# Moving GLU, gates and a branch between attention heads, and building SSM rotations from tables

## The chip, the cores and the metric

The kernel runs on one core of one Trainium2 chip. The time is device microseconds of one launch, from runs that each compute the whole layer; lower is better. A profile is one further execution, recorded by the hardware profiler. Engines are named as in the profile: PE (TensorE, matmuls), PEld (its weight loads), DVE (VectorE), ACT (ScalarE), POOL (GpSimd), SP (SyncE, which here issues most DMAs).

## The reference

One layer of a decoder over 1024 tokens with 16 meta tokens ahead of them (1040 positions, width 1024), all in float32:

```
xn = RMSNorm(h);  [q | k | v | u | gate_a | gate_b] = xn @ W_in
a  = stick-breaking attention(q, k, v)     8 heads x 64, strictly causal
     z = q.k / 8;  w[t,s] = sigmoid(z[t,s]) * prod over s<j<t of sigmoid(-z[t,j]);  a = w @ v
y  = gelu(S5(u))                           32 groups x 16 channels, 64 complex states each
     x_t = lam x_(t-1) + B u_t;  S5 = Re(C x_t) + D u_t
s  = y * sigmoid(y @ W_glu + b)
h += (sigmoid(gate_a) * (a @ W_pa) + sigmoid(gate_b) * (s @ W_pb)) @ W_o
h += MoE(RMSNorm(h))                       top 1 of 4 groups, top 2 of its 8 experts
out = RMSNorm(h), meta tokens dropped
```

## The kernel before

**Matmuls in two parts.** Operands are split into a rounded high part (type float32r) and the rest as a low part. `split` (L99) makes both: a cast on ACT and a subtraction on DVE. `mm3` (L132) then does three matmuls, high by high, high by low, low by high. `load_w` (L144) loads a block of weights through a buffer `wr` (two of them) and splits it; the parts go to `wh` and `wl`, two buffers each.

**Order of the work.** A tile framework orders the instructions of each engine ahead of time by a simulated timeline, and follows the order of the program as a priority; what runs on the chip is that fixed order with semaphores. The program is written with generators. `weave(main, fill, n_main, n_fill)` (L57) takes one step of the main work and then so many of the fill that both come out even; `drain` runs one to its end. The stages, in the order of the program:

- The norm of all 1040 positions gives `xh` and `xl` (the transposed input in two parts, 66 KB a partition together), which stay until the last projection is done. `ssm_in` projects `u` and sends it to memory.
- `ssm_prep` (L370) computes on DVE, in many small operations of 32 elements, the powers of the state's decay, the tables `BA`, `BB`, `C1`, `C2`, and `c`, `s`: cosine and sine of the angle of eight steps.
- `ssm` (L515) handles four blocks of eight groups. The sequence is cut into chunks of eight positions, so a state runs over 129 chunk steps. A block's rotations `RC`, `RS` (cosine and sine of 0 to 128 such angles) are built on POOL by doubling: seven rounds of six products and sums (L549 to L554). Then DVE builds `GT` and `ET`, PE transposes and multiplies (L569, L577), SP copies `KP` into the eight shifted bands of `M`, PE multiplies the input (L598), DVE rotates the result with `RC` and `RS` (L600 to L603), scans it (L606), POOL and DVE rotate it back (L608 to L611), PE makes the output (L618, L620), which goes through a gelu to memory (`y_d`).
- `gates` (L176) is 16 projections in 32 steps, each 24 matmuls of 512 columns, a sigmoid and a store to `gate_d`. Twenty-one steps are woven into the SSM's 24 (SF = 21), three stand after it (MF = 3), the other eight among the first three head pairs (GP = 3, 3, 2).
- Attention works on four pairs of heads. `att_proj` (L669) projects q, k and v of a pair in eight steps. For q the 64 rows of a head are followed by the 64 rows of its low part, so `qs` has 128 rows; the high part of k stands twice in `k1`, its low part twice in `k2`. `att_pair` (L727) has 16 steps: two heads, four double blocks of queries, two steps each. A chunk of scores is two matmuls over 128 rows (L745 with `k1`, L746 with `k2`); then two sigmoids on ACT, masks on POOL (L751), the running product on DVE (L754), the weights on POOL (L755), transposes on PE (L770), a split, and the product with V (L790; L785 in the last pair, without low parts). The 16 meta tokens are a key block of their own, with matmuls of 16 rows. Into each of the first three pairs the next pair's projection and the gate steps are woven.
- The last pair takes its first step, then the remaining gate steps run, `xh` and `xl` are freed, and `glu` (L632) is woven into the pair: it loads `y_d`, splits it, does eight products of 12 matmuls and writes the parts of s to `sh`, `sl`. The attention's results of the other pairs are loaded from memory (`attn_d`) into `ah`, `al`.
- The branch loop (L334) does, for each of eight column blocks, the SSM's part (24 matmuls), the attention's part (24) and the products with the gates. Then come the output projection with the router, and 32 experts.

Of the kernel before, what the change touches and what calls it, by code (L numbers as in the profile page):

```python
# [44 lines left out]
SF, MF, GP = 21, 3, (3, 3, 2)  # L45
# [28 lines left out]
def tile_block(ctx, tc, i, out):  # L74
# [64 lines left out]
    with ExitStack() as ca:  # L139
# [21 lines left out]
        with ExitStack() as cx:  # L161
# [120 lines left out]
            next(pair)  # L282
            drain(gen)
            cq.close()


        with ExitStack() as c4:
# [3 lines left out]
            with ExitStack() as c6:  # L291
                nc.sync.dma_start(gb, i["glu_b"])
                at = pool(c6, "glu", bufs=2, side="right")
                gl = glu(tc, at, ps, i, load_w, mm3, split, gb, y_d, sh, sl)

                def loads():
                    for k in range(3):
                        a = wp.tile([128, 2, 512], F32, name="wr", bufs=2)
                        nc.sync.dma_start(a, attn_d[k * 128:k * 128 + 128])
                        split(ah[:, k], al[:, k], a.rearrange("p a b -> p (a b)"))  # L300
                        yield
# [32 lines left out]
            for m in range(KD):  # L334
                h, l = load_w([wb[:, :, m * 128:m * 128 + 128], wa[:, :, m * 128:m * 128 + 128]])
                T2 = []
                for q in range(2):
                    c = slice(q * 512, q * 512 + 512)
                    t = ps.tile([128, 512], F32, name="qk", bufs=2)
                    for k in range(4):  # L340
                        mm3(t, h[:, k, :], l[:, k, :], sh[:, k, c], sl[:, k, c], k == 0, k == 3)
# [28 lines left out]
def ssm_prep(tc, p, i, bcast, out):  # L370
# [144 lines left out]
def ssm(tc, p, ps, ident, u_d, y_d, prep):  # L515
# [9 lines left out]
    for blk in range(4):  # L525
# [876 lines left out]
```

## Time and profile before

| | |
|---|---|
| three runs, median (lowest to highest) | 1538.57 us (1536.74 to 1539.53) |
| the profiled execution, its own time | 1539.6 us |
| its span, first to last instruction | 1537.7 us |
| mean granted clock of TensorE | 0.974 |
| DVE, ACT, POOL busy | 63%, 47%, 34% |
| SSM stage, about | 73 to 272 us |
| four head pairs, about | 285 to 652 us |
| branch, output projection, router | 655 to 864 us |
| experts and the end | 864 to 1538 us |

The profile's matmuls overlap (the end of one is modelled), so the distance between two starts says what a matmul costs, not its length. A row of the timeline gives its start, its length, the engine, line and operation, what it writes and reads with its size, how many like it follow, and in brackets the engine's idle time before it and what ended it. `128*128 128x512` is a matmul of 128 rows by 128 columns of weights, with 128x512 moving elements.

### The profile page before, as it was taken

To read this page: it belongs to the slowest core of one execution; us is meant where nothing else is said; L and a number is where in the kernel's file an instruction comes from. 1 tells how busy PE (TensorE), PEld (TensorE's weight loads), DVE (VectorE), ACT (ScalarE), POOL (GpSimd) and SP (SyncE) were. 2 spreads that over 40 slices of the span, in tenths; PEclk is the share of its full clock that TensorE was granted. 3 is DMA by queue.
4 is the path that set the end of the run, shared out by engine and by line. 5 is a ranking of instruction groups with operands and counts; after the bars stand their busy time and mean duration, and the time that the engine had idled before them with its cause. 6 is when DMAs were issued, how large, how long until landed. Compare 5 with 4: busy or idle time off the path is not lost. (4 is left out here: it accounts for less than half of the span.)

```text
span 1537.7 us, 19509 instructions
## 1 busy us (share of the span) xinstructions
PE 1456.8 (95%) x6900; PEld 1123.4 (73%) x6900; DVE 963.0 (63%) x1488; ACT 722.3 (47%) x1141; POOL 518.9 (34%) x542
## 2 busy tenths in 40 slices
PE   7989799999999989999998799999999999999986
PEld 6967688998888867778787566666666666666663
DVE  6757565465756568665578566666665566656547
ACT  6212122455656577432223255555555455555543
POOL 1199941144444465332255321111111111111034
PEclk8999899999999999999999799999999999999998
DMA  8242344211111015264763799999999989999754
GB/s 256 77 104 72 92 104 97 60 42 54 30 51 34 28 44 142 78 198 160 268 247 124 286 346 356 352 354 353 356 360 351 353 342 358 334 334 357 271 200 163
DMA packets 132197, 314.77 MB, mean 205 GB/s; under 512 B 24305, under 2 KB 82289, under 8 KB 107522
## 3 DMA queue, kind: packets, MB, share of 16 engines
q1 hardware_dynamic: 120898, 295.99, 55.0%
q0 software_dynamic: 9728, 16.83, 2.9%
q8 instruction: 55, 0.90, 0.2%
q10 hardware_dynamic: 1472, 0.69, 0.2%
q14 instruction: 44, 0.36, 0.1%
HBM read 284.03 MB, written 44.11 MB: 213 GB/s over the span
## 5 line engine op out<-in xcount | busy, mean ns | idle before, releaser
L134 PE MATMUL mm<-xh,wh 128*128 128x512 f32 (+4 forms) x608 | 224.1, 369 | 1.1 <-DVE kl L691 0.6
L135 PE MATMUL mm<-xl,wh 128*128 128x512 f32 (+4 forms) x608 | 222.6, 366 | 0.0
L136 PE MATMUL mm<-xh,wl 128*128 128x512 f32 (+4 forms) x608 | 221.3, 364 | 0.8 <-DVE wl L102 0.8
L1159 POOL DMA_INDIRECT ye_d<-w,tab x32 | 56.1, 1754 | 250.0 <-ACT w L1152 249.4
L134 PEld LDWEIGHTS mm<-xh,wh 128*128 128x128 f32 x608 | 115.4, 190 | 16.0 <-issue 1.1
L136 PEld LDWEIGHTS mm<-xh,wl 128*128 128x128 f32 x608 | 115.4, 190 | 14.9 <-DVE wl L102 1.5
L135 PEld LDWEIGHTS mm<-xl,wh 128*128 128x128 f32 x608 | 115.3, 190 | 13.9 <-DVE xl L225 0.4
L754 DVE TENSOR_TENSOR_SCAN pr<-pr 128x144 f32<-128x144 f32 (+3 forms) x64 | 92.6, 1448 | 46.8 <-POOL pr L751 46.1
L102 DVE TENSOR_TENSOR w<-m,w 128x2048 fp32r<-128x2048 f32 x38 | 88.9, 2342 | 40.8 <-ACT w L101 40.7
L102 DVE TENSOR_TENSOR w<-r,w 128x2048 fp32r<-128x2048 f32 x36 | 82.2, 2291 | 47.6 <-ACT w L101 47.2
L1066 POOL DMA_INDIRECT w<-hg_d,tab x31 | 34.8, 1122 | 222.0 <-PE tr L1088 217.1
L755 POOL TENSOR_TENSOR be<-be,pr 128x143 f32<-128x143 f32 (+3 forms) x64 | 89.4, 1400 | 38.4 <-DVE pr L754 36.0
L1120 PE MATMUL a<-r,xf 128*128 128x512 f32 x224 | 100.7, 592 | 0.0
L1120 PE MATMUL a<-m,xf 128*128 128x512 f32 x208 | 93.3, 592 | 0.0
L1128 DVE SCALAR_TENSOR_TENSOR mid<-a,tab,mid 128x512 f32<-128x512 f32 x64 | 47.9, 749 | 63.8 <-ACT mid L1126 52.0
L101 ACT CAST w<-r 128x2048 fp32r<-128x2048 f32 x38 | 72.1, 1903 | 27.5 <-PE a L1113 14.4
L101 ACT CAST w<-m 128x2048 fp32r<-128x2048 f32 x38 | 72.5, 1907 | 18.9 <-PE o L1146 10.3
L101 ACT CAST wh<-wr 128x1024 fp32r<-128x1024 f32 (+1 forms) x44 | 44.6, 1014 | 65.8 <-PE mm L135 57.3
L1120 PEld LDWEIGHTS a<-r,xf 128*128 128x128 f32 x224 | 41.8, 190 | 42.3 <-issue 40.4
L102 DVE TENSOR_TENSOR wl<-wr,wh 128x1024 fp32r<-128x1024 f32 (+1 forms) x44 | 57.1, 1297 | 23.6 <-ACT wh L101 23.5
L1146 PE MATMUL o<-w,w 128*128 128x512 f32 x172 | 68.6, 399 | 3.2 <-DVE w L102 3.2
L751 POOL TENSOR_SCALAR_AFFINE_SELECT pr<-pr 128x128 f32<-128x128 f32 x64 | 26.3, 411 | 132.9 <-ACT pr L748 113.1
(534 smaller groups left out, 3766.2 us busy)
## 6 DMA issues: line engine op xcount, KB each, us to landing
r<-in_w_dram SPq DMA_DIRECT2D x84, 1024.0 KB, 7.9
m<-in_w_dram SPq DMA_DIRECT2D x82, 1024.0 KB, 8.1
x<-in_w_dram SPq DMA_DIRECT2D x26, 1024.0 KB, 7.9
wr<-in_w_in_dram SPq DMA_DIRECT2D x32, 512.0 KB, 4.2
gate_d<-gt SPq DMA_DIRECT2D x32, 256.0 KB, 2.3
x<-in_x_dram SPq DMA_DIRECT2D x8, 512.0 KB, 4.6
y<-y_d SPq DMA_DIRECT2D x16, 256.0 KB, 3.2
wr<-in_w_out_dram SPq DMA_DIRECT2D x8, 512.0 KB, 4.3
```

The source lines that it names most:

```text
L101: a = (A if heng is None else heng).copy(h, src)
L102: return a.ins, (V if leng is None else leng).tensor_sub(l, src, _f(h)).ins
L134: nc.tensor.matmul(ps, lhsT=wh, rhs=xh, start=first, stop=False)
L135: nc.tensor.matmul(ps, lhsT=wh, rhs=xl, start=False, stop=False)
L136: nc.tensor.matmul(ps, lhsT=wl, rhs=xh, start=False, stop=last)
L754: V.tensor_tensor_scan(rv, rv, rv, 1.0, op0=OP.mult, op1=OP.bypass)
L755: P.tensor_mul(be[:, :W - 1], be[:, :W - 1], pr[:, 1:W])
L1066: q = P.indirect_dma_start(out=xg[e % XG], out_offset=None, in_=hg_d, in_offset=IO(ap=tab[:, e, 0:1] if e else rt["idx"], axis=0), bounds_ ...
L1120: nc.tensor.matmul(a[w], lhsT=xf[:, k], rhs=raws[n][:, k], start=False, stop=(k == 3))
L1128: V.scalar_tensor_tensor(s, a[n], r, s, op0=OP.mult, op1=OP.mult)
L1146: nc.tensor.matmul(o[n], lhsT=hh[:, kk], rhs=l[:, k, cs], start=False, stop=False)
L1159: put = P.indirect_dma_start(out=ye_d, out_offset=IO(ap=tab[:, e, 1:2], axis=0), in_=y, in_offset=None, bounds_check=2 * S - 1, oob_is_err ...
```

## The change

It does five things. The GLU runs earlier: it is loaded in the middle of the first pair's projection, and its eight products are the first fill of the first pair, followed by the second pair's projection and one gate step (17 fill steps in 16); its result goes to memory (`s_d`) instead of `sh`, `sl`. The three gate steps between the SSM and attention go; pairs 0, 1 and 2 have 1, 3 and 3, and the first half of the last pair has four (GL). In the second half of the last pair s is loaded and split, and the SSM's part of the first two column blocks is done (AHEAD = 2), with products of the gates kept in `gb`; the branch loop starts the others itself. The low part of k is kept once, each head in its own 64 rows, and L746 multiplies it with the 64 rows of q's high part, so the product of the two low parts is no longer formed. The rotations come from two tables made once in `ssm_prep`, `pb` (0 to 16 angles) and `pa` (0 to 8 times 16 angles), by one complex product over 8 x 9 x 16 elements a block: the sine's three operations on DVE, the cosine's three on POOL. Beside that, `M` is two tiles cleared once, `KP` has half its size, `ET` one buffer in place of two, and the first head's result of the last pair goes through `attn_d`.

```diff
-SF, MF, GP = 21, 3, (3, 3, 2)
+SF, GP, GL = 21, (1, 3, 3), 4
+AHEAD = 2
...
+    s_d = dr.tile([512, S], F32, name="s_d")
...
-            aq = [None, pool(c3, "aq1", bufs=2)]
-            cq = ExitStack()
-            aq[0] = pool(cq, "aq0", bufs=2)
+            aq = [pool(c3, "aq0", bufs=2), None]
+            cg = ExitStack()
+            nc.sync.dma_start(gb, i["glu_b"])
+            gl = glu(tc, pool(cg, "glu", bufs=2, side="right"), ps, i, load_w, mm3, split, gb, y_d, s_d)
             st = {}
-            drain(islice(gen, MF), att_proj(tc, ap, aq[0], ps, proj, ident, 0, st))
+            pr0 = att_proj(tc, ap, aq[0], ps, proj, ident, 0, st)
+            drain(islice(pr0, 4))
+            next(gl)
+            drain(pr0)
+
+            def ahead():
+                yield from gl
+                cg.close()
+                aq[1] = pool(c3, "aq1", bufs=2)
+                yield from att_proj(tc, ap, aq[1], ps, proj, ident, 1, st)
+
             for hp in range(3):
                 pair = att_pair(tc, ap, ps, ident, hp, st, attn_d)
-                fill = chain(att_proj(tc, ap, aq[(hp + 1) % 2], ps, proj, ident, hp + 1, st), islice(gen, GP[hp]))
-                weave(pair, fill, 16, 8 + GP[hp])
+                nx = ahead() if hp == 0 else att_proj(tc, ap, aq[(hp + 1) % 2], ps, proj, ident, hp + 1, st)
+                fill = chain(nx, islice(gen, GP[hp]))
+                weave(pair, fill, 16, 8 + GP[hp] + (8 if hp == 0 else 0))
                 drain(fill, pair)
+
             dst = []
             pair = att_pair(tc, ap, ps, ident, 3, st, attn_d, dst)
-            next(pair)
+            weave(pair, gen, 8, GL)
             drain(gen)
-            cq.close()
+            cx.close()
...
-            with ExitStack() as c6:
-                nc.sync.dma_start(gb, i["glu_b"])
-                at = pool(c6, "glu", bufs=2, side="right")
-                gl = glu(tc, at, ps, i, load_w, mm3, split, gb, y_d, sh, sl)
...
-                dst += ah, al
-                weave(pair, chain(gl, loads()), 16, 18)
-                drain(pair, gl)
+            pg = pool(c5, "gat", side="right", bufs=2)
+            wa = i["w_branch_attn"].rearrange("(k p) c -> p k c", p=128)
+            wb = i["w_branch_ssm"].rearrange("(k p) c -> p k c", p=128)
+            wu, parts = {}, {}
+
+            def load_s(src, h_, l_, k, n):
+                a = wp.tile([128, 2, 512], F32, name="wr", bufs=2)[:n]
+                nc.sync.dma_start(a, src[k * 128:k * 128 + n])
+                split(h_[:n, k], l_[:n, k], a.rearrange("p a b -> p (a b)"))
+
+            def ssm_part(m, nm):
+                wu[m] = load_w([wb[:, :, m * 128:m * 128 + 128], wa[:, :, m * 128:m * 128 + 128]])
+                h, l = wu[m]
+                for q in range(2):
+                    c = slice(q * 512, q * 512 + 512)
+                    g_ = parts[m, q] = pg.tile([128, 512], F32, name="gb", bufs=2 + 2 * AHEAD)
+                    nc.sync.dma_start(g_, gate_d[D + m * 128:D + m * 128 + 128, c])
+                    t = ps.tile([128, 512], F32, name=nm, bufs=2)
+                    for k in range(4):
+                        mm3(t, h[:, k, :], l[:, k, :], sh[:, k, c], sl[:, k, c], k == 0, k == 3)
+                    V.tensor_mul(g_, g_, t)
+                    yield
+
+            def early():
+                for k in range(4):
+                    load_s(s_d, sh, sl, k, 128)
+                    yield
+                for m in range(AHEAD):
+                    yield from ssm_part(m, "mm")
+                for k in range(3):
+                    load_s(attn_d, ah, al, k, 128)
+                    yield
+                load_s(attn_d, ah, al, 3, 64)
+                yield
+
+            dst += ah, al
+            fill = early()
+            weave(pair, fill, 8, 8 + 2 * AHEAD)
+            drain(pair, fill)
...
+                if m >= AHEAD:
+                    drain(ssm_part(m, "qk"))
+                h, l = wu[m]
...
+                    ga, g_ = pg.tile([128, 512], F32, name="ga"), parts[m, q]
...
+    f1, f2 = BA[:, :, 0:8], BA[:, :, 8:16]
+
+    def powers(nm, top, r1, i1):
+        R, I = W(nm + "r", (128, G, top + 1)), W(nm + "i", (128, G, top + 1))
+        V.memset(R[:, :, 0:1], 1.0)
+        V.memset(I[:, :, 0:1], 0.0)
+        V.tensor_copy(R[:, :, 1], r1)
+        V.tensor_copy(I[:, :, 1], i1)
+        n = 1
+        while n < top:
+            a, b = f1[:, :, :n], f2[:, :, :n]
+            ar, ai = R[:, :, 1:n + 1], I[:, :, 1:n + 1]
+            br, bi = (x[:, :, n:n + 1].to_broadcast([128, G, n]) for x in (R, I))
+            V.tensor_mul(a, ai, bi)
+            V.tensor_mul(b, ar, br)
+            V.tensor_sub(R[:, :, n + 1:2 * n + 1], b, a)
+            V.tensor_mul(a, ar, bi)
+            V.tensor_mul(b, ai, br)
+            V.tensor_add(I[:, :, n + 1:2 * n + 1], a, b)
+            n *= 2
+        return R, I
+
+    pb = powers("pb", 16, c, s)
+    pa = powers("pa", 8, pb[0][:, :, 16], pb[1][:, :, 16])
...
-        RC, RS = W("RC", (128, 8, N), bufs=2), W("RS", (128, 8, N), bufs=2)
-        P.memset(RC[:, :, 0:1], 1.0)
-        P.memset(RS[:, :, 0:1], 0.0)
-        P.tensor_copy(RC[:, :, 1], c[:, gs])
-        P.tensor_copy(RS[:, :, 1], s[:, gs])
-        ta, tb = W("ta", (128, 8, 64)), W("tb", (128, 8, 64))
-        n = 1
-        while n < 128:
-            br, bi = (x[:, :, n:n + 1].to_broadcast([128, 8, n]) for x in (RC, RS))
-            ar, ai = RC[:, :, 1:n + 1], RS[:, :, 1:n + 1]
-            a, b = ta[:, :, :n], tb[:, :, :n]
-            P.tensor_mul(a, ai, bi)
-            P.tensor_mul(b, ar, br)
-            P.tensor_sub(RC[:, :, n + 1:2 * n + 1], b, a)
-            P.tensor_mul(a, ar, bi)
-            P.tensor_mul(b, ai, br)
-            P.tensor_add(RS[:, :, n + 1:2 * n + 1], a, b)
-            n *= 2
+
+        RC, RS = (W(n, (128, 8, 9, 16), bufs=2) for n in ("RC", "RS"))
+        ta, tb = W("ta", (128, 8, 9, 16)), W("tmp", (128, 8, 9, 16))
+        (ar, ai), (br, bi) = ([x[:, gs, :9, None].to_broadcast([128, 8, 9, 16]) for x in pa],
+                              [x[:, gs, None, :16].to_broadcast([128, 8, 9, 16]) for x in pb])
+        for eng, R, t, x, y, op in ((V, RS, tb, (ar, bi), (ai, br), OP.add), (P, RC, ta, (ar, br), (ai, bi), OP.subtract)):
+            eng.tensor_mul(R, *x)
+            eng.tensor_mul(t, *y)
+            eng.tensor_tensor(R, R, t, op=op)
+        RC, RS = (x.rearrange("p g a b -> p g (a b)")[:, :, :N] for x in (RC, RS))
...
-        GT, tmp, ET = W("GT", (128, 8, T + 1, CH), bufs=2), W("tmp", (128, 8, T + 1, CH)), W("ET", (128, 8, T, CH), bufs=2)
+        GT, tmp, ET = W("GT", (128, 8, T + 1, CH), bufs=2), W("tmp", (128, 8, T + 1, CH)), W("ET", (128, 8, T, CH))
...
-        M = W("M", (128, 8, 128), bufs=2)
-        KPf = KP.rearrange("p g a b -> p g (a b)")
+        V.tensor_add(KP[:, :, 0:CH], KP[:, :, 0:CH], dg)
+        M = Ms[blk % 2]
         for ti in range(T):
-            nc.sync.dma_start(M[ti * CH:ti * CH + CH], KPf[:, :, 128 - CH * ti:256 - CH * ti])
+            nc.sync.dma_start(M[ti * CH:ti * CH + CH, :, CH * ti:], KP[:, :, :128 - CH * ti])
...
-            split(sh[:, m, c], sl[:, m, c], sg.rearrange("p c t -> p (c t)"))
+            nc.sync.dma_start(s_d[m * 128:m * 128 + 128, q * 512:q * 512 + 512], sg.rearrange("p c t -> p (c t)"))
...
-        k2 = [pq.tile([128, L], F32R, name="kl", bufs=2) for _ in range(2)]
+        k2 = pq.tile([128, L], F32R, name="kl", bufs=1)
...
-                V.tensor_sub(k2[e][a, n0:n1], t[a, :n], _f(k1[e][a, n0:n1]))
-                V.tensor_sub(k2[e][b, n0:n1], t[a, :n], _f(k1[e][a, n0:n1]))
+                V.tensor_sub(k2[a, n0:n1], t[a, :n], _f(k1[e][a, n0:n1]))
...
+            own = slice(64 * e, 64 * e + 64)
...
-                        nc.tensor.matmul(z[:, :c1 - c0], lhsT=q, rhs=k2[e][:, c0:c1], start=False, stop=True)
+                        nc.tensor.matmul(z[:, :c1 - c0], lhsT=q[own], rhs=k2[own, c0:c1], start=False, stop=True)
...
-                c = slice(j * 256, j * 256 + 256)
-                if dst is None:
-                    ao = p.tile([64, 256], F32, name="ao")
-                    A.copy(ao, po[64:128, :])
-                    V.tensor_add(ao, po[0:64, :], ao)
-                    nc.sync.dma_start(attn_d[(2 * hp + e) * 64:(2 * hp + e) * 64 + 64, c], ao)
+                c, row = slice(j * 256, j * 256 + 256), (2 * hp + e) * 64
+                if dst:
+                    ah, al = dst
+                    A.copy(ah[own, hp, c], po[own])
+                    V.tensor_sub(al[own, hp, c], po[own], _f(ah[own, hp, c]))
                 else:
-                    ah, al = dst
-                    r = slice(64 * e, 64 * e + 64)
-                    A.copy(ah[r, hp, c], po[r])
-                    V.tensor_sub(al[r, hp, c], po[r], _f(ah[r, hp, c]))
+                    ao = p.tile([128, 256], F32, name="ao")[own if dst is not None else slice(0, 64)]
+                    if dst is None:
+                        A.copy(ao, po[64:128, :])
+                        V.tensor_add(ao, po[0:64, :], ao)
+                    else:
+                        A.copy(ao, po[own])
+                    nc.sync.dma_start(attn_d[row:row + 64, c], ao)
```

## Rows read from the trace of the kernel before

**Rows 1.** Page, engines: busy us (share of the span) and instructions.
```profile
PE 1456.8 (95%) x6900; PEld 1123.4 (73%) x6900; DVE 963.0 (63%) x1488; ACT 722.3 (47%) x1141; POOL 518.9 (34%) x542
```

**Rows 2.** Windows by stage: length, busy us per engine, granted clock, DMA share, GB/s.
```profile
54.70:102.00 47.30, 47.30 (x245) 41.56 (x244) 40.54 (x152) 10.20 (x16) 27.75 (x38) 1.00 0.33 102
73.40:272.00 198.60, 180.38 (x892) 147.98 (x891) 123.90 (x162) 45.84 (x71) 134.37 (x197) 0.94 0.41 97
108.50:121.00 12.50, 5.56 (x16) 4.61 (x16) 7.88 (x15) 0.00 (x0) 11.17 (x26) 0.59 0.17 32
170.10:186.00 15.90, 5.92 (x30) 5.93 (x30) 3.54 (x4) 0.81 (x2) 14.83 (x29) 0.57 0.11 33
272.00:545.00 273.00, 270.07 (x1605) 237.99 (x1604) 168.44 (x251) 156.87 (x385) 112.42 (x135) 1.00 0.14 41
545.00:572.00 27.00, 21.28 (x113) 16.46 (x114) 17.30 (x26) 17.16 (x49) 18.03 (x24) 0.87 0.12 38
572.00:655.00 83.00, 79.88 (x393) 62.49 (x392) 59.89 (x57) 50.46 (x117) 36.80 (x36) 1.00 0.36 106
```

**Rows 3.** Timeline of TensorE, SSM stage: start, length, instruction, idle time before.
```profile
115.45 0.77 PE L598 MATMUL qk<-U,E 128*128 128x129 f32 x2 [6.94 <-DVE mm__1124 L602]
...
180.10 0.77 PE L618 MATMUL qk<-R,GT 128*128 128x128 f32 x2 [9.98 <-DVE R L611]
```

**Rows 4.** Timeline of VectorE, just before those two.
```profile
110.64 0.56 DVE L600 TENSOR_TENSOR R<-qk,RC 128x387 f32<-128x387 f32 x1 [8.53 <-POOL RC L551]
...
178.66 1.29 DVE L611 SCALAR_TENSOR_TENSOR R<-mm__1464,nsgn,R 128x1032 f32<-128x1032 f32 x1 [12.79 <-POOL R L608]
```

**Rows 5.** Lines of GpSimd, 67 to 207 us: count, busy us, mean ns, idle.
```profile
L551 POOL TENSOR_TENSOR RC<-tb,ta 128x8 f32<-128x8 f32 (+6 forms) x28 | 21.6, 773 | 2.0
...
L552 POOL TENSOR_TENSOR ta<-RC,RS 128x8 f32<-128x8 f32 (+6 forms) x28 | 16.6, 593 | 2.0
L608 POOL TENSOR_TENSOR R<-St,RC 128x1032 f32<-128x1032 f32 x2 | 4.8, 2396 | 0.0
```

**Rows 6.** Lines of VectorE by form, 54 to 102 us.
```profile
L558 DVE TENSOR_TENSOR GT<-C,Lr 128x1152 f32<-128x1152 f32 x2 | 2.7, 1356 | 0.0
...
L503 DVE TENSOR_TENSOR BA<-X,fr 128x512 f32<-128x512 f32 x1 | 0.7, 684 | 0.0
...
L454 DVE TENSOR_TENSOR Li<-t,t 128x128 f32<-128x128 f32 x1 | 0.3, 291 | 0.0
...
L454 DVE TENSOR_TENSOR Li<-t,t 128x32 f32<-128x32 f32 x1 | 0.2, 200 | 0.0
```

**Rows 7.** Timeline of TensorE around one matmul of 16 rows.
```profile
352.27 0.40 PE L136 MATMUL mm<-xh,wl 128*128 128x512 f32 x1
352.50 0.39 PE L134 MATMUL mm<-xh,wh 128*128 128x512 f32 x1
352.82 0.38 PE L790 MATMUL pv<-wth,V 16*128 16x256 f32 x1
353.13 0.51 PE L135 MATMUL mm<-xl,wh 128*128 128x512 f32 x1
353.48 0.40 PE L136 MATMUL mm<-xh,wl 128*128 128x512 f32 x1
```

**Rows 8.** Lines of VectorE, whole span.
```profile
L691 DVE TENSOR_TENSOR kl<-mm,kh 64x344 fp32r<-64x344 f32 (+1 forms) x24 | 12.4, 516 | 0.3
...
L102 DVE TENSOR_TENSOR al<-wr,ah 128x1024 fp32r<-128x1024 f32 x3 | 4.5, 1491 | 1.6 <-ACT ah L101 1.6
```

**Rows 9.** DMA issues, 540 to 660 us: count, KB each, us to landing.
```profile
wr<-attn_d SPq DMA_DIRECT2D x3, 512.0 KB, 3.4
```

**Rows 10.** Lines of TensorE, 276 to 655 us.
```profile
L746 PE MATMUL qk<-kl,qs 128*128 128x264 f32 (+6 forms) x112 | 36.2, 326 | 0.0
```

**Rows 11.** Timeline of TensorE around a transpose of 16 columns.
```profile
367.78 0.27 PE L770 MATMUL tr<-ident,be 128*16 128x128 f32 x1
367.80 0.36 PE L790 MATMUL pv<-wtl,V 128*128 128x256 f32 x1
```

More of the change, by code (lines that the diff above doesn't have):

```diff
@@ L159, in tile_block @@
         ei = con.tile([128, 128], I32, name="ei")
-        with ExitStack() as cx:
+        cx = ExitStack()
+        if True:
             xp = pool(cx, "xp", side="right")
@@ L290, in tile_block @@
             ah, al, sh, sl = (p.tile([128, 4, S], F32R, name=n) for n in ("ah", "al", "sh", "sl"))
-            with ExitStack() as c6:
-                nc.sync.dma_start(gb, i["glu_b"])
-                at = pool(c6, "glu", bufs=2, side="right")
-                gl = glu(tc, at, ps, i, load_w, mm3, split, gb, y_d, sh, sl)
[L296 to L301, printed above, removed]
-                dst += ah, al
-                weave(pair, chain(gl, loads()), 16, 18)
-                drain(pair, gl)
+            pg = pool(c5, "gat", side="right", bufs=2)
@@ L353, in tile_block @@
                     V.tensor_mul(ga, ga, t)
-                    P.tensor_add(ga, ga, gb)
+                    P.tensor_add(ga, ga, g_)
                     for r in range(2):
@@ L442, in ssm_prep @@
     V.tensor_mul(Li[:, 1], mag, s)
-    t1, t2 = W("t1", (128, 4, G)), W("t2", (128, 4, G))
+    BA, BB = (W(n, (128, G, CH)) for n in ("BA", "BB"))
+    t1, t2 = (BB.rearrange("p g c -> p (g c)")[:, n * 4 * G:(n + 1) * 4 * G].rearrange("p (a g) -> p a g", a=4) for n in range(2))
     n = 1
@@ L489, in ssm_prep @@
     yield
-    X, X2, C1, C2, BA, BB, u1 = (W(n, (128, G, CH)) for n in ("X", "X2", "C1", "C2", "BA", "BB", "u1"))
+    X, X2, C1, C2, u1 = (W(n, (128, G, CH)) for n in ("X", "X2", "C1", "C2", "u1"))
     for x, x2, src in ((X, X2, i["b"]), (C1, C2, i["c"])):
@@ L510, in ssm_prep @@
     V.tensor_scalar(C2, C2, -1.0, None, op0=OP.mult)
-    out.update(c=c, s=s, Lr=Lr, Li=Li, d8=d8, BA=BA, BB=BB, C1=C1, C2=C2, sg=sg, nsg=nsg, dd=dd)
+    out.update(pa=pa, pb=pb, Lr=Lr, Li=Li, d8=d8, BA=BA, BB=BB, C1=C1, C2=C2, sg=sg, nsg=nsg, dd=dd)
 def ssm(tc, p, ps, ident, u_d, y_d, prep):
@@ L517, in ssm @@
     V, A, P = nc.vector, nc.scalar, nc.gpsimd
-    c, s, Lr, Li, d8, BA, BB, C1, C2, sg, nsg, dd = (
-        prep[n] for n in ("c", "s", "Lr", "Li", "d8", "BA", "BB", "C1", "C2", "sg", "nsg", "dd"))
+    pa, pb, Lr, Li, d8, BA, BB, C1, C2, sg, nsg, dd = (
+        prep[n] for n in ("pa", "pb", "Lr", "Li", "d8", "BA", "BB", "C1", "C2", "sg", "nsg", "dd"))
     def W(name, shape=(128, G), dt=F32, bufs=1):
@@ L524, in ssm @@
     N = NCH - 1
+    Ms = [W(f"M{n}", (128, 8, 128)) for n in range(2)]
+    for M in Ms:
+        P.memset(M, 0.0)
     for blk in range(4):
@@ L570, in ssm @@
             A.copy(E[:, g0:g0 + 4], tp)
-        KP = W("KP", (CH, 8, 2, 128))
-        P.memset(KP[:, :, 0], 0.0)
+        KP = W("KP", (CH, 8, 128))
         for g0 in (0, 4):
@@ L629, in ssm, with glu @@
                                         ap=[[S, CH], [CH * S, 8], [1, 128]]), Y[ti * CH:ti * CH + CH])
-def glu(tc, p, ps, i, load_w, mm3, split, gb, y_d, sh, sl):
+def glu(tc, p, ps, i, load_w, mm3, split, gb, y_d, s_d):
     nc = tc.nc
@@ L659, in glu @@
                 mm3(t, h[:, k, :], l[:, k, :], y4[0][:, k], y4[1][:, k], k == 0, k == 3)
-            sg = p.tile([128, 64, T], F32, name="sg", bufs=1)
+            sg = p.tile([128, 64, T], F32, name="sg", bufs=2)
             A.activation(sg, t.rearrange("p (t c) -> p c t", t=T), AF.Sigmoid, bias=gb[:, m:m + 1])
             V.tensor_mul(sg, sg, y.rearrange("p t c -> p c t"))
-            c = slice(q * 512, q * 512 + 512)
-            split(sh[:, m, c], sl[:, m, c], sg.rearrange("p c t -> p (c t)"))
+            nc.sync.dma_start(s_d[m * 128:m * 128 + 128, q * 512:q * 512 + 512], sg.rearrange("p c t -> p (c t)"))
             yield
```

18 lines of the change are left out of this document (1 added, 17 removed).

## The prediction

> **What bounds the kernel now.** I read the page's engine table first: TensorE is busy 95% of the span, no other engine above 63% [rows 1]. So the kernel is as long as TensorE's work, plus the time in which it stands still, plus what it loses at the lower clock. Next the windows by stage [rows 2], to see where it stands still. Between 272 and 545 us (projections and the first head pairs) TensorE is busy 270.07 of 273 us: nothing done there on other engines can shorten it. It stands still in two other places. One is the SSM stage, 73.4 to 272 us: 198.6 - 180.38 = 18.2 us idle. Two holes make 16.9 of it, 6.94 us before 115.45 and 9.98 us before 180.10 [rows 3]; around each the granted clock falls to 0.59 and 0.57 of full, that is, part of the stretch runs at 1.2 in place of 2.4 GHz [rows 2]. The lanes behind the holes name GpSimd: VectorE waited 8.53 us for RC and 12.79 us for the product R of L608 [rows 4], and L608 is issued on GpSimd among the rotations, with GpSimd busy 14.83 of the 15.9 us around the second hole [rows 2]. The other place is the end of the attention: 27 - 21.28 = 5.7 us idle in 545 to 572, with the clock at 0.87, and 3.1 us in 572 to 655.
>
> What stands still is the most that can be won. The clock: in 108.5 to 121 us the 5.56 busy us came after the hole, nearly all at half speed, and 5.92 us after the second one, so about 2.7 us are lost twice. That makes 18.2 + 5.4 = 23.6 us in the SSM stage. In 545 to 572 a mean of 0.87 over 27 us means 2 x 0.13 x 27 = 7 us at half speed, 3.5 lost; 5.7 + 3.5 + 3.1 = 12.3 us at the attention's end.
>
> **Part 1, rotations from short tables.** GpSimd loses six groups of 28 products and sums each (the first and the last of the six in [rows 5]): 21.6 + 20.3 + 18.9 + 18.5 + 17.7 + 16.6 = 113.6 us. It gains three operations over 1152 elements a block; L608 over 1032 takes 2.40 us [rows 5], so 2.7 us each, 8 us a block, 32 in all, and two memsets. VectorE gains the other three of each block at 1.36 us (L558, the same 1152 elements [rows 6]): 4.1 x 4 = 16.3 us. It gains the tables too: four doublings for pb and three for pa, six operations each over 32, 64, 128 and 256 elements. 0.20 us is the row for 32 elements, 0.29 that for 128 and 0.68 that for 512 [rows 6]; with 0.20, 0.23, 0.29 and 0.42 (the second and the fourth lie between rows) pb costs 6.8 us and pa 4.3, and eight copies and memsets 1.2: 12.3 us. These stand in the preparation, where VectorE is already busy 40.5 of 47.3 us [rows 2] and TensorE has only matmuls that need none of it, so nothing ends later at once; but the first block's tables come about 12 us later.
>
> So the stage changes its second engine. TensorE has less to do there, as three gate steps (72 matmuls at 0.23 us [rows 7], 16.6 us) leave it: 180.4 - 16.6 - 5.4 = 158 us, to 73.4 + 158 = 232 us. VectorE has 123.9 + 12.3 + 16.3, less 1.5 weight halves at 1.2 us: 151 us, to 224 us if it never waits, and to 241 us at a busy share of 0.9 (62% before). Both end between 232 and 245 us. I take 8 us of idle time and lost clock where 23.6 stood: **-15 us**, bounds -23.6 and 0.
>
> **Part 2, GLU beside the first heads and through memory; gates and the SSM's branch at the end.** These move matmuls and add none. The GLU's casts into sh and sl become a store of 2 MB and four loads with a cast and a subtraction of 1.49 us (the al row [rows 8]) in place of eight smaller ones; a load of this size lands in 3.4 us [rows 9]. SP and the DMA engines have room (share 0.14 [rows 2]), and pair 0 gets 17 fill steps where it had 11, so it is TensorE that ends last there. What is won is the hole of 545 to 572, which four gate steps now fill, and the GLU's waits for its split inputs. What is late next is the middle of the last pair: xh and xl must be free before sh and sl exist; then four loads and splits run through two buffers, 2 x (3.4 + 1.5 us + a cast) or some 13 us, in which TensorE has only the pair. In 545 to 572 the pair alone kept it 79% busy, so 13 x 0.21 = 2.7 us, and some 2 us of clock: 5 us in place of 12.3, **-7 us**, bounds -12 and +8 (a second hole of that kind). In the branch loop the weights of m + 2 still wait for the matmuls of m, as before: 0, bounds -1 and +3.
>
> **Part 3, keys' low parts once.** VectorE loses 24 subtractions of 0.52 us, 12.4 us (L691 [rows 8]), where it was not the bound: 0. SBUF is saved, which costs and gives no time itself. But the second score matmul (L746) changes its shape: it read 128 rows, now the 64 rows of its head. There are 112 [rows 10], and each stands between matmuls of 128 rows. No row of before has a matmul of 64 rows. The nearest rows are those of 16 rows, on the meta tokens. In [rows 7] a 16-row matmul of 256 columns starts at 352.82. The 512-column matmul before it holds TensorE 0.32 us (normal 0.23), the short one itself 0.31 (256 columns at full height need half of 0.23), the next one 0.35. From 352.50 to 353.48 is 0.98 us where 0.23 + 0.12 + 0.23 = 0.58 would do: 0.40 us lost around one short matmul, none of it as idle time. Bounds for 64 rows: 0 (the height matters only below some size) and 0.40 us; I take 0.40, as the loss falls before, in and after the short matmul, as if the array had first to empty and then load weights in the open. 112 x 0.40 = 45 us. The scores are computed in stretches where TensorE has no free time (2.9 of 273 us [rows 2]), so little hides it; I let a tenth vanish in the holes left: **+40 us**, bounds 0 and +45.
>
> The Trainium skill, TensorEngine Tiling (Array Packing), section Key Properties, says that a change of the tiling mode, not only of the tile, makes TensorE drain, and it counts 64 rows as a mode of its own. By that rule the 0.40 us of [rows 7] applies to 64 rows too, and the trace agrees as far as 16 rows go. The page TensorE: Matmul & The Clock Gate, section Why this matters for your kernels, says that one matmul of 32 rows takes as long as one of 128; by that the term would be nothing, and [rows 7] contradict it whenever such a matmul stands alone.
>
> **Sum.** The profiled execution took 1539.6 us with a span of 1537.7; the median of the runs is 1538.57, 1.0 below it. 1539.6 + 40 - 15 - 7 = 1557.6 us, on the scale of the runs **1557 us**, 1.2% slower.
>
> **Rivals.**
> A, the other side: a matmul of 64 rows costs no switch. For it: only 16-row matmuls show one, and columns cut to 16 show none (the matmul after the 128*16 transpose of [rows 11] starts 0.02 us after it). Against: the loss sits in the neighbours, where the number of rows should not matter. Then 1538.6 - 15 - 7 = 1517 us. It decides from 22 / (112 x 0.9) = 0.22 us a matmul: below that the kernel gets faster. A smaller loss in proportion lies between.
> B, half of the switch is paid, say the way in or the way out, as the 64-row weights can be loaded early: 20 us, 1538.6 + 20 - 22 = 1537 us, no change that can be measured.
> C, VectorE becomes the SSM stage's bound: 12.3 + 16.3 us come to it, three gate steps leave TensorE, and the order on each engine is fixed beforehand. For it: its work (151 us) and TensorE's (158 us) are nearly equal. Against: GpSimd's 113.6 us were in the way of VectorE as well. Then the stage's holes stay as they are, and the time is 1557 + 15 = 1572 us.
>
> **How the numbers follow.** The forecast has a chance of 0.50 (its own range 1546 to 1568: +35 to +45 for the rows, -22 to -10 for the SSM stage, -12 to -2 for the end of the attention), A 0.26, B 0.13, C 0.11. The low end, 1512 us, takes in A with -15 and -12; the high end, 1573 us, takes in C. About 0.1 is left out on either side, for A with everything won (1503 us) and for C with a new hole. A measurement tells 0.2%, 3 us, from no change. Faster: A, and a fifth of B, 0.28. Same: half of B and the edges, 0.08. Slower: the forecast, C and the rest of B, 0.64.
>
> **What would show each step.** Switch: L746 as 64*128, the matmul before it 0.09 us longer than its columns need, the one after 0.1 us; the stretch of the four pairs longer by some 40 us with TensorE still busy throughout. If the matmul before L746 and the one after keep their spacing, A is right. SSM stage: the L549 to L554 groups gone, no hole of 7 or 10 us, the stage over by 250 us (272 before). Attention's end: no hole at 545 to 572, a shorter one in the last pair where sh and sl are loaded. I am wrong if the time is below 1538 us, and wrong in the cause if it is above while L746's neighbours are undisturbed.

## The result, and the profile after

The changed kernel takes 1585.94 us (median of 4 runs, 1584.89 to 1587.63) against 1538.51 us (4 runs, 1536.74 to 1539.53): ratio 1.0311, 95% interval 1.0293 to 1.0328. It is 47 us slower where 18.5 us had been forecast. The direction was right; the size was far out, and the time lies above the range of 1512 to 1573 us.

The page's engine row of the changed kernel, beside [rows 1]:

```profile
PE 1497.3 (95%) x6900; PEld 1130.3 (71%) x6900; DVE 992.5 (63%) x1519; ACT 727.4 (46%) x1138; POOL 449.0 (28%) x368
```

TensorE has the same 6900 matmuls and is again busy 95%, but for 40 us longer; GpSimd lost 70 us of work, VectorE got 30. Next the windows by stage of the changed kernel (columns as in [rows 2]: stretch, length, busy us of PE, PEld, DVE, ACT and POOL, granted clock, DMA share, GB/s):

```profile
73.40:105.00 31.60, 31.60 (x139) 25.62 (x138) 29.17 (x47) 6.66 (x9) 19.13 (x8) 1.00 0.36 101
105.00:121.00 16.00, 8.23 (x35) 5.78 (x34) 15.79 (x10) 3.30 (x5) 5.69 (x2) 0.79 0.21 66
121.00:186.00 65.00, 60.39 (x313) 48.79 (x312) 62.43 (x71) 14.92 (x24) 23.41 (x7) 0.99 0.36 91
186.00:255.00 69.00, 66.94 (x361) 55.84 (x360) 54.46 (x75) 16.82 (x27) 8.41 (x10) 0.99 0.39 94
255.00:285.00 30.00, 18.47 (x78) 17.18 (x78) 13.81 (x21) 12.84 (x27) 3.07 (x6) 0.72 0.35 99
285.00:630.00 345.00, 344.15 (x1812) 273.72 (x1811) 189.47 (x257) 184.84 (x444) 138.90 (x155) 1.00 0.19 55
630.00:655.00 25.00, 21.99 (x88) 15.44 (x88) 18.92 (x14) 15.97 (x33) 15.67 (x15) 0.86 0.59 190
655.00:702.00 47.00, 43.60 (x185) 31.49 (x183) 15.56 (x15) 19.15 (x51) 17.64 (x18) 0.89 0.13 36
```

Three things are to be seen. From 285 to 630 us TensorE hardly stands still (0.85 us in all), and yet the heads take longer. In 105 to 121 us VectorE is busy 15.79 of 16 us: it has taken GpSimd's place as the engine that TensorE waits for in the SSM stage. And 255 to 285 us is new: 11.5 us idle at a clock of 0.72, where the kernel before has one hole of 0.43 us. Its window and that hole (columns as in [rows 2] and [rows 3]):

```profile
255.00:285.00 30.00, 29.57 (x159) 25.86 (x158) 13.69 (x21) 9.65 (x16) 0.34 (x2) 1.00 0.31 88
```

```profile
281.16 0.40 PE L134 MATMUL mm<-xh,wh 128*128 128x344 f32 x1 [0.43 <-DVE qs L682]
```

The timeline of TensorE in the changed kernel gives the holes:

```profile
111.90 0.51 PE L138 MATMUL mm<-xh,wl 128*128 128x512 f32 x1 [4.49 <-DVE wl L104]
115.69 1.11 PE L620 MATMUL tr<-ident,ET 128*128 128x128 f32 x4 [3.28 <-DVE ET L614]
...
184.72 0.77 PE L667 MATMUL qk<-R,GT 128*128 128x128 f32 x2 [2.60 <-DVE R L660]
...
259.91 0.66 PE L136 MATMUL mm<-xh,wh 128*128 128x352 f32 x1 [6.97 <-DVE qs L730]
...
268.48 0.40 PE L136 MATMUL mm<-xh,wh 128*128 128x344 f32 x1 [1.67 <-DVE qs L730]
...
278.44 0.63 PE L136 MATMUL mm<-xh,wh 128*128 128x344 f32 x1 [3.87 <-DVE kl L738]
```

Of the holes of [rows 3], as forecast, the one of 6.94 us is gone, and 2.60 of the 9.98 us are left at the same place (before 184.72: the same matmul, which is L618 before and L667 now). The others are new. The last three belong to the first projection of attention. Why it waits, the queues of ScalarE and then VectorE show (changed kernel, same columns):

```profile
256.40 0.63 ACT L674 ACTIVATE qq<-qq 128x512 f32<-128x512 f32 x1 [1.28 <-DVE qq L673]
256.93 1.04 ACT L729 CAST qs<-mm 64x512 fp32r<-64x512 f32 x2
...
266.26 0.62 ACT L103 CAST yh<-y 128x512 fp32r<-128x512 f32 x1 [7.13 <-DMA y<-y_d]
266.90 0.58 ACT L729 CAST qs<-mm 64x512 fp32r<-64x512 f32 x1
```

```profile
257.06 0.69 DVE L675 TENSOR_TENSOR Y<-qq,qk 128x512 f32<-128x512 f32 x1 [0.70 <-ACT qq L674]
257.78 2.08 DVE L730 TENSOR_TENSOR qs<-mm,qs 64x512 fp32r<-64x512 f32 x3
266.91 0.69 DVE L104 TENSOR_TENSOR yl<-y,yh 128x512 fp32r<-128x512 f32 x1 [7.06 <-ACT yh L103]
267.64 0.69 DVE L730 TENSOR_TENSOR qs<-mm,qs 64x512 fp32r<-64x512 f32 x1
```

The first evictions of q (the cast L729 and the subtraction L730, which empty an accumulator) stand behind the last SSM block's gelu (L674, L675), so TensorE waits 6.97 us for a free accumulator. Later ones stand behind the GLU's first casts (L103), which wait for `y`, just written to memory by that same block. In the kernel before, three gate steps covered the first of these waits (experiment 6).

### The profile page after: what moved, and what is told of

Read it like the earlier page. It is cut to its first block, busy times and chain, and to the rows that moved or that the text cites. A ratio compares the mean times of both kernels' runs of the same rounds, so it can differ in the third digit from the quotient of the medians.

```text
span 1582.9 us, 19381 instructions
## 1 busy us (share of the span) xinstructions
PE 1497.3 (95%) x6900; PEld 1130.3 (71%) x6900; DVE 992.5 (63%) x1519; ACT 727.4 (46%) x1138; POOL 449.0 (28%) x368
## 5 line engine op out<-in xcount | busy, mean ns | idle before, releaser
L136 PE MATMUL mm<-xh,wh 128*128 128x512 f32 (+4 forms) x608 | 225.9, 372 | 12.8 <-DVE qs L730 8.6
L138 PE MATMUL mm<-xh,wl 128*128 128x512 f32 (+4 forms) x608 | 224.6, 370 | 5.3 <-DVE wl L104 5.3
L803 POOL TENSOR_TENSOR be<-be,pr 128x143 f32<-128x143 f32 (+3 forms) x64 | 85.7, 1341 | 22.6 <-DVE pr L802 19.2
L103 ACT CAST w<-r 128x2048 fp32r<-128x2048 f32 x38 | 72.1, 1903 | 27.4 <-PE a L1163 14.3
L103 ACT CAST w<-m 128x2048 fp32r<-128x2048 f32 x38 | 72.5, 1908 | 18.9 <-PE o L1196 10.3
L104 DVE TENSOR_TENSOR wl<-wr,wh 128x1024 fp32r<-128x1024 f32 (+1 forms) x44 | 61.9, 1408 | 28.9 <-ACT wh L103 28.8
L799 POOL TENSOR_SCALAR_AFFINE_SELECT be<-be 128x128 f32<-128x128 f32 x64 | 63.6, 994 | 52.1 <-ACT be L797 41.5
L103 ACT CAST wh<-wr 128x1024 fp32r<-128x1024 f32 (+1 forms) x44 | 44.5, 1011 | 70.9 <-PE mm L137 59.6
L796 ACT ACTIVATE pr<-qk 128x144 f32<-128x144 f32 (+6 forms) x112 | 50.7, 454 | 52.8 <-PE qk L794 41.8
```

The lines of the kernel that those rows point to most:

```text
L103: a = (A if heng is None else heng).copy(h, src)
L104: return a.ins, (V if leng is None else leng).tensor_sub(l, src, _f(h)).ins
L136: nc.tensor.matmul(ps, lhsT=wh, rhs=xh, start=first, stop=False)
L138: nc.tensor.matmul(ps, lhsT=wl, rhs=xh, start=False, stop=last)
L796: A.activation(pr[:, c0:c1], z[:, :c1 - c0], AF.Sigmoid, scale=-HD ** -0.5)
L799: P.affine_select(out=w[:, W - 128:W], in_=w[:, W - 128:W], pattern=[[-1, 128]], base=0, channel_multiplier=1, compare_op=OP.is_gt, fill=fill)
```

## The experiments

Ratios are to the kernel before on the same chip, with 95% intervals; its median was 1538.81 us in experiments 1 to 4, 1540.25 in 5 to 8 and 1539.26 in 9 to 12. Ratios are compared across sets, times within one.

**1. All rows in the changed kernel.**

```diff
-lhsT=q[own], rhs=k2[own, c0:c1]
+lhsT=q, rhs=k2[:, c0:c1]
```

This is the second score matmul, L746 before and L794 in the changed kernel. Its other 64 rows now add a product of two low parts, q's by the other head's keys.

> The changed kernel, with the one matmul of L794 on all 128 rows (lhsT=q, rhs=k2[:, c0:c1]); the other 64 rows then add the low part of the queries by the other head's low keys, nothing that counts. Theory 1 (the 64-row matmul costs its two switches, 72 seen at +94.5 and +107 ns and some 112 in all, so about 44 us, and the other parts together gain next to nothing): 1586 - 44 = 1542, at most 2 us either way. Rival A (rows switch for nothing, the +46 us come from the order of the GLU, gates and branch): 1584 to 1588. Rival B (half the price stays): 1564.

Measured 1558.75 us (1556.89 to 1560.52), 1.0132 (1.0117 to 1.0148). None of the expectations, rival B's 1564 us being the nearest: the 64 rows cost 27 us, not 44 and not nothing, and 20 us of the loss have nothing to do with them.

**2. 64 rows in the kernel before**, with the same edit the other way round (`q` and `k2[e]` cut to the head's 64 rows).

> The kernel before, with only L746 on its own head's 64 rows (the same keys' tiles, still written twice). Theory 1: 1538.5 + 112 x 0.39 = 1582, within 3 us. Rival A: 1538 to 1540. Rival B: 1560.

Measured 1565.64 us (1562.99 to 1569.67), 1.0173 (1.0157 to 1.0189): 26.8 us, again between rival B and theory 1. Both kernels give 27 us, 0.24 us a matmul. What it is, the timeline of TensorE in the changed kernel shows around one such matmul (start, length, instruction):

```profile
354.57 0.33 PE L137 MATMUL mm<-xl,wh 128*128 128x352 f32 x1
354.74 0.28 PE L793 MATMUL qk<-kh,qs 128*128 128x264 f32 x1
354.95 0.38 PE L794 MATMUL qk<-kl,qs 64*128 64x264 f32 x1
355.26 0.43 PE L138 MATMUL mm<-xh,wl 128*128 128x352 f32 x1
355.54 0.32 PE L136 MATMUL mm<-xh,wh 128*128 128x352 f32 x1
355.70 0.32 PE L137 MATMUL mm<-xl,wh 128*128 128x352 f32 x1
```

From start to start: 264 columns at 128 rows take 0.21 us where about 0.12 would do, those at 64 rows 0.31, the 352 columns after it 0.28 where 0.16 is normal (355.54 to 355.70): 0.09 + 0.19 + 0.12 = 0.40 us around one matmul, as in [rows 7]. This one is typical. Taking the starts of both traces against the usual distance for the same number of columns (an estimate), a short matmul among 128-row ones, with no idle time beside it, loses 0.39 us in the median: 47 matmuls of 64 rows in the changed kernel, 13 of 16 rows in the kernel before. What the whole is worth is less. One row each for the stretch from the second head of pair 0 to the second head of the last pair (84 of the 112), first of experiment 1, then of the changed kernel:

```profile
334.50:612.50 278.00, 275.01 (x1588) 236.74 (x1587) 165.49 (x224) 163.08 (x399) 129.32 (x146) 0.99 0.20 59
```

```profile
336.20:638.70 302.50, 301.01 (x1588) 237.50 (x1586) 167.59 (x222) 165.42 (x398) 131.17 (x145) 1.00 0.17 53
```

The same 1588 matmuls take 24.5 us longer, 0.29 us for each of the 84; TensorE's busy time grew by 26 us, while 1.5 us of idle time and the last of the lost clock (0.99 to 1.00, up to 2.8 us) went. In the kernel before and in experiment 2 it is the same:

```profile
340.30:587.90 247.60, 239.28 (x1391) 204.15 (x1390) 159.93 (x226) 149.96 (x381) 124.05 (x146) 0.99 0.14 43
```

```profile
346.30:614.90 268.60, 265.80 (x1391) 207.48 (x1390) 162.13 (x227) 151.45 (x381) 125.69 (x147) 0.99 0.13 39
```

21 us longer (0.25 us each), 26.5 us busier (0.32 each), 5.5 us less idle: holes that ended on other engines disappear when TensorE itself comes later. The Trainium skill, TensorEngine Tiling (Array Packing), section Key Properties, has TensorE drain at a change of mode; these rows agree so far as time is lost around each matmul of 64 rows, and they give the price.

**3. The tables alone**: the kernel before with the changed `ssm_prep` and `ssm`.

> The kernel before, with only the SSM's preparation and blocks of the changed one (rotations from two short tables, one KP, two standing M). My forecast's term: -15, so 1523. Theory 1 (the stage's idle time only moves: 4.5 + 3.3 + 1.9 + 2.6 = 12.3 us of holes that end on VectorE stand in place of 18.2 that ended on GpSimd, and here three gate steps still lie over the stage's end): 1530 to 1536. Rival C (VectorE is now the bound and its operations run at twice their time beside GpSimd's, so the stage is later than before): 1540 to 1548.

Measured 1533.64 us (1531.35 to 1534.37), 0.9961 (0.9947 to 0.9974): 5.2 us faster, within theory 1.

**4. The moves alone**: experiment 1 with the `ssm_prep` and `ssm` of the kernel before. The keys' low parts are still kept once here; experiment 12 finds nothing measurable in that.

> The changed kernel with all 128 rows in L794 and the SSM's preparation and blocks of the kernel before: so only the moves of GLU, gates and branch, and the low keys written once. My forecast's term for the moves: -7, so 1531. Theory 1 (the moves only shift idle time, the three gate steps that no longer follow the SSM uncover its end): 1538 to 1550, because GpSimd then ends the SSM later under the first projection. Rival D (the moves lose what the tables gain): over 1550.

Measured 1564.28 us (1560.69 to 1566.75), 1.0162 (1.0147 to 1.0178): 25.5 us slower, past theory 1 and in rival D. Against experiment 1 the tables are again worth 5.5 us. Rows, tables and moves as steps from one kernel to the other, 27.2 - 5.5 + 25.5 = 47.2, give the whole by construction; that the parts really add up is seen from the kernel before, where rows and tables alone measured 26.8 and -5.2: 26.8 - 5.2 + 25.5 = 47.1. The moves, forecast as a gain, cost as much as the rows.

**5. Cover for the end of the SSM stage**: experiment 1 with three gate steps put back.

```diff
-SF, GP, GL = 21, (1, 3, 3), 4
+SF, MF, GP, GL = 21, 3, (0, 2, 2), 4
...
-            drain(islice(pr0, 4))
+            drain(islice(gen, MF), islice(pr0, 4))
```

> The kernel with all 128 rows in the second score matmul (1558.75 us), with three gate steps taken out of the first three pairs (GP from 1, 3, 3 to 0, 2, 2) and put back behind the SSM blocks, ahead of the first projection. Theory 2 (the moves cost their time mainly where the SSM stage ends: without these steps TensorE stands 6.97 + 3.19 + 4.13 + 0.75 + 0.90 = 15.9 us while the first projection's evictions queue behind the SSM's last blocks, and some 5 us of clock with it): the first score matmul starts where it does now plus 0 to 3 us, the pairs are 15.6 us shorter, 1541 to 1546. Rival E (the moves cost it in the last pair, where the clock is half in three stretches, 8 to 11 us): the holes behind the SSM go, but come back in the pairs; 1555 to 1560.

Measured 1538.96 us (11 runs, 1534.80 to 1544.49), 0.9990 (0.9978 to 1.0001): about 22 us by the ratios (1.0132 - 0.9990), a little more than theory 2 said. The stretch where the SSM stage ends, in experiment 1 and then here:

```profile
255.00:296.00 41.00, 26.55 (x133) 25.63 (x134) 16.71 (x27) 17.82 (x37) 4.91 (x9) 0.79 0.31 84
```

```profile
255.00:292.00 37.00, 32.42 (x186) 29.19 (x185) 19.22 (x29) 19.81 (x39) 2.71 (x6) 1.00 0.40 114
```

Idle time falls from 14.5 to 4.6 us, and the clock comes back from 0.79 to 1.00: 0.79 over 41 us is 2 x 0.21 x 41 = 17 us at 1.2 GHz, up to 8.6 us lost. (The two profiled executions are 15 us apart, the medians 20.)

**6. The same undone in the kernel before** (MF 3 to 0, GP 3, 3, 2 to 4, 4, 3).

> The kernel before, with its three gate steps behind the SSM moved into the first three pairs (MF 3 to 0, GP 3, 3, 2 to 4, 4, 3), nothing else. Theory 2: holes of 7, 2 and 4 us wait for qs and kl ahead of the first score matmul, and the clock falls: 1538.5 + 14 to 20 = 1553 to 1558. Rival E: 1538 to 1542, as the pairs take the steps as well as the SSM's end does.

Measured 1563.69 us (1561.58 to 1565.81), 1.0155 (1.0141 to 1.0169): 23.4 us slower, more than expected. Its TensorE timeline:

```profile
269.02 0.66 PE L134 MATMUL mm<-xh,wh 128*128 128x352 f32 x1 [6.92 <-DVE qs L682]
...
572.18 1.24 PE L770 MATMUL tr<-ident,be 128*16 128x128 f32 x5 [4.09 <-POOL be L755]
```

The hole for `qs` is there, but not the two after it; here no cast of the GLU stands in ScalarE's queue at that place. The rest of the loss is later. The first score matmul starts at 279.4 us (285.0 before) with three gate steps, 16.6 us, less ahead of it, so about 11 us are lost up to there. From it to the first matmul of the output projection it is 466.8 us (440.1 before), 10 us more than the three steps that came in; the largest hole there is the 4.09 us before 572.18. I had not expected the order there to change with three steps, and which of its waits matter stays open. So this run shows that the steps behind the SSM are worth over 20 us in this kernel too, and that about half of it is lost at that place.

**7. Two more gate steps for the last pair**, from pairs 1 and 2 of experiment 5 (GP 0, 1, 1, GL 6).

> As the kernel with three gate steps behind the SSM, with two more steps taken out of pairs 1 and 2 (GP 0, 1, 1) and put into the first half of the last pair (GL 4 to 6). Theory 2 with its second part (the last pair's first half has too little beside it: 1.8 us idle and 4.7 us lost at half clock): 3 to 6 us faster than that kernel, 1537 to 1541. Rival G (pairs 1 and 2 need their three steps as much): the same as that kernel within 2 us, holes of some 0.5 to 1.5 us in pairs 1 and 2.

Measured 1545.05 us (9 runs, 1542.38 to 1547.91), 1.0033 (1.0023 to 1.0043): 6 us slower than experiment 5, where theory 2 said faster and rival G the same. Pairs 1 and 2 show holes, as rival G said, and larger ones than it said (experiment 5 has one of 1.80 us in pair 2), and the last pair is not better filled either (the wait before 608.88):

```profile
475.04 0.39 PE L838 MATMUL pv<-wtl,V 128*128 128x256 f32 x1 [1.94 <-DVE wtl L829]
480.44 0.43 PE L136 MATMUL mm<-xh,wh 128*128 128x352 f32 x1 [0.97 <-DVE qs L730]
500.60 0.61 PE L818 MATMUL tr<-ident,be 128*16 128x128 f32 x4 [1.99 <-POOL be L803]
...
608.88 0.50 PE L138 MATMUL mm<-sh,wl 128*128 128x512 f32 x1 [3.06 <-DVE wl L104]
```

**8. The tables with GpSimd left out**: experiment 3 with the products of RC on VectorE (`(P, RC, ...)` becomes `(V, RC, ...)`).

> The kernel before with the tables (1533.64 us), with the products for RC on VectorE too, in place of GpSimd. Theory 3 (the tables gained 5 and not 15 us because a VectorE operation that meets one of GpSimd takes 3.2 in place of 1.2 to 1.36 us, 12 such operations of RC): VectorE gets 12 x 1.36 = 16 us and loses 12 x 1.9 = 23 us of waiting, and the holes at 114.03 and 117.82 (4.49 and 3.00 us, behind GpSimd's products at 97 to 113 us) shrink to under 4 us together: 1526 to 1532. Rival F (VectorE's amount of work is the bound of this stage, 139 of 160 us): 1540 to 1550.

Measured 1526.77 us (1524.73 to 1530.29), 0.9909 (0.9894 to 0.9924): 0.5% below experiment 3, and faster than both kernels. The timelines of experiment 3, GpSimd and then VectorE, show why:

```profile
106.65 3.67 POOL L575 TENSOR_TENSOR RC<-RC,ta 128x1152 f32<-128x1152 f32 x1
110.40 2.50 POOL L574 TENSOR_TENSOR ta<-pai,pbi 128x1152 f32<-128x1152 f32 x1
```

```profile
107.72 3.15 DVE L534 TENSOR_TENSOR BB<-BB,u 128x512 f32<-128x512 f32 x1
110.79 3.19 DVE L102 TENSOR_TENSOR wl<-wr,wh 128x1024 fp32r<-128x1024 f32 x1
113.90 1.34 DVE L581 TENSOR_TENSOR GT<-GT,tmp 128x1152 f32<-128x1152 f32 x1
```

And VectorE here, where GpSimd has no RC to make:

```profile
104.08 0.68 DVE L534 TENSOR_TENSOR BB<-BB,u 128x512 f32<-128x512 f32 x1
...
110.89 1.22 DVE L102 TENSOR_TENSOR wl<-wr,wh 128x1024 fp32r<-128x1024 f32 x1
```

The same operation over 512 elements takes 3.15 us beside GpSimd and 0.68 alone, the one over 1024 3.19 and 1.22. The windows from 73.4 us to the first score matmul, experiment 3 and then this one:

```profile
73.40:280.00 206.60, 194.12 (x974) 159.92 (x973) 172.88 (x225) 50.14 (x79) 56.63 (x25) 0.97 0.36 95
```

```profile
73.40:270.30 196.90, 191.99 (x974) 159.73 (x973) 164.03 (x236) 49.95 (x79) 15.55 (x13) 0.98 0.37 99
```

VectorE does 11 more instructions in its window and is busy 8.9 us less; TensorE's idle time falls from 12.5 to 4.9 us. The Trainium skill, SBUF — State Buffer, section SBUF: two separate sides, says that a GpSimd operation and a VectorE operation with two SBUF inputs share a pair of ports, and whichever starts second is blocked for the whole of the other; these rows agree.

The kernel before has this meeting too, in the last two blocks of the SSM; [rows 5] end ahead of them. GpSimd, then VectorE, there:

```profile
214.85 3.42 POOL L608 TENSOR_TENSOR R<-St,RC 128x1032 f32<-128x1032 f32 x1 [3.23 <-DVE St L606]
```

```profile
214.74 1.23 DVE L609 TENSOR_TENSOR mm__1798<-St,RS 64x1032 f32<-64x1032 f32 x1
215.98 3.38 DVE L610 TENSOR_TENSOR mm__1798<-St,RS 64x1032 f32<-64x1032 f32 x1
```

In the first two blocks L608 meets no VectorE operation and takes 2.45 and 2.35 us, and L610 takes 1.34 and 1.56.

**9. Cover in the changed kernel itself**, 64 rows and all, with the edit of experiment 5 alone.

> The changed kernel as it is, 64 rows and all, with the three gate steps back behind the SSM (MF 3, GP 0, 2, 2). Theory 2 with the switch at 27 us (the parts add up: 27 for the rows, some 20 of the 25 for the bare end of the SSM stage): 1586 - 20 = 1566, 1563 to 1569. Rival H (the bare end of the SSM stage and the switches share idle time, so that they don't add): 1570 to 1576.

Measured 1570.97 us (1569.14 to 1575.80), 1.0206 (1.0187 to 1.0225): 16 us by the ratios, in rival H. The cover and the switch don't quite add up: with the rows switching it is worth 16, without 22.

**10. Cover, 128 rows and RC on VectorE**: experiment 5 with the edit of 8.

> The kernel with 128 rows and the three gate steps behind the SSM (1538.96 us), with the products for RC on VectorE. Theory 3 (GpSimd's operations hold VectorE up): as in the kernel before, 7 us: 1532, 1529 to 1535. Rival F: within 2 us of 1539, because this order has the GLU's work near the SSM's end.

Measured 1533.04 us (1532.42 to 1535.19), 0.9961 (0.9948 to 0.9975): theory 3, though holes of 4.91 and 4.28 us at the SSM stage's end are back; I put them down to the stage being over earlier, which no run tests. This is the moved version at its best here; it is as fast as the tables alone (experiment 3) and slower than experiment 8.

**11 and 12. A fourth gate step behind the SSM** (experiment 8 with SF 20, MF 4), **and the low keys once, on all 128 rows** (experiment 8 with one `kl`).

> The kernel before with tables, all on VectorE (1526.77 us), with a fourth gate step behind the SSM, taken out of the 21 beside its blocks. Theory 2 (the end of the SSM stage needs TensorE work until the last block is out; one hole of 4.91 us is left there): 3 to 6 us less, 1521 to 1524. Rival I (the 21 steps beside the blocks are needed there as much): 1526 to 1530.

> The kernel before with tables, all on VectorE (1526.77 us), with the keys' low parts written once and read on all 128 rows. My forecast's step (12.4 us of VectorE where it is not the bound: 0): 1525 to 1528. Rival J (the evictions of the keys are on the path, L691 releases TensorE in two holes of 0.4 and 0.6 us): 2 to 4 us less.

Measured 1522.57 us (1522.09 to 1525.79), 0.9897 (0.9881 to 0.9912), and 1523.11 us (1521.77 to 1526.98), 0.9896 (0.9879 to 0.9914). The ratio of experiment 8 is 0.9909, and the intervals overlap: inconclusive both, 0.12 and 0.13% apart from it. The fourth step did little at the hole that it was meant for: 4.32 us are left of 4.91. They are the fastest versions here, 1% below the kernel before.

## Why the prediction was right or wrong

The terms of the forecast, rows, tables and moves, were +40 - 15 - 7 = +18 us; measured are +27.2 - 5.5 + 25.5 = +47.2. So the moves missed by 32.5 us and the tables by 9.5, and it is luck that the rows, 12.8 us below their term, made up part of it. (The three ranges given for the forecast add up to 1540 to 1572 us, wider than its 1546 to 1568; the measured time is above either.)

**The view of the bound** held. Between 285 and 630 us nothing but TensorE's own work counts, and what was added there was paid.

**Part 3, the rows, +40 us: mechanism right, size off; 27 measured.** The 0.40 us around one short matmul is what [rows 7] foretold, in the same three places, and 64 rows switch as 16 do. Rival A, the likeliest way to a gain, is out. The step that failed is "I let a tenth vanish in the holes left": 0.24 of 0.40 us remained. By the stretch of experiment 2, TensorE is busy 0.32 us longer for each, and idle time gives 5.5 / 84 = 0.07 of that back. The forecast also counted the whole 0.40 as new. By the starts in that stretch (the estimate of experiment 2, idle time left out), the 84 matmuls and their neighbours take about 0.42 us each more than their columns need with 64 rows, but 0.09 already with 128, so 0.33 are new. Part of the 0.09 is the loss beside 16-row matmuls, where 6 of the 84 stand; the rest is not taken apart.

**Part 1, the tables, -15 us: too much; 5 measured.** That the holes behind GpSimd go was right, but for 2.60 us. The step that failed is "VectorE gains the other three of each block at 1.36 us", with 2.7 us for GpSimd's: both are durations of operations that nothing held up. In the changed kernel the three lines of GpSimd take 2.9 to 4.0 us in the mean, and of the 13 VectorE operations that start while one of them runs 11 take 2.2 to 3.8 us. [rows 6] are themselves from a stretch with GpSimd busy, so they did not warn of it; L608 and L610 after 207 us do (experiment 8), and so does the page of the Trainium skill named there. Experiment 8 measures the term with the meeting taken away: about 14 us (0.9%), near the forecast. Rival C named the engine; its mechanism, the amount of work, was not the cause: with more instructions on VectorE the stage got faster.

**Part 2, the moves, -7 us: wrong in sign; +25.5 measured.** Two steps failed. The first is in part 1's sum: "TensorE has less to do there, as three gate steps (...) leave it". I counted their leaving as a gain to the stage and never asked what they hid. They stood over the last block's gelu and the first projection's evictions; experiment 5 gives back 22 us of the 25.5 with them. The second is "pair 0 gets 17 fill steps where it had 11, so it is TensorE that ends last there": true of the pair, but the GLU's loads come at the projection ahead of it, and its casts wait on ScalarE for `y` (7.13 us) with q's evictions queued behind them. I had named no queue there. The trace shows this second wait; no run moves the GLU's load alone, so its price by itself is not measured.

At the end of attention the hole of 545 to 572 us did go, and a sparser stretch came later: 3.0 us idle in 630 to 655 and 3.4 in 655 to 702, at clocks of 0.86 and 0.89, up to 3.5 and 5.2 us more: 15 where the prediction counted 12.3 before. No run takes that stretch apart, so which wait makes it stays open.

With the cover back the moves still cost 4.5 us (0.9990 in experiment 5 against 0.9961 in 3). The timeline of experiment 5 has one hole ahead of the first score matmul that experiment 3 has not:

```profile
278.22 0.50 PE L793 MATMUL qk<-kh,qs 128*128 128x144 f32 x2 [3.29 <-ACT kh L737]
```

There the casts of k stand behind the GLU's casts on ScalarE, as above. Whether this hole is what is left of the loss, no run tests.

## What to carry to other kernels

Work that is moved away leaves what it covered: before pricing a move, read which engine is late at the old place, and which evictions queue there. A shape of matmul that alternates with another costs its switches every time, and that they show as busy and not as idle time makes them easy to miss. A duration read from one engine's row holds only as long as the other engine does what it did in that row; when work is put on GpSimd beside VectorE, price both as they are together.

## What was not expected of the hardware

Elementwise operations with both inputs in SBUF take 3.2 us on VectorE in place of 0.7 to 1.2 when they start while one runs on GpSimd (experiment 8), so that 12 operations more on VectorE made it less busy by 9 us. And the lower clock takes a share that the idle time does not show: in experiment 1 the 14.5 us of holes came with 17 us of the stretch at 1.2 GHz, and with three gate steps the clock was 1.00 and 4.6 us of the holes were left.
